# A three-block sequence model on one core: the sequence in two halves, one behind the other through all blocks

## The chip, the cores and the metric

The kernel runs on one core of a Trainium2 chip. The metric is the device time of one execution in microseconds (us). Inputs and weights lie in device memory (HBM). All arithmetic is in float32; the large products split both factors into a high and a low part of the type fp32r and add three products (high·high, high·low, low·high).

## The reference

The input has 1024 tokens of 1024 channels; 16 learned tokens go in front (1040 columns in the kernel's transposed layout). Two layers (a mixer, then a feed-forward block) and a second block follow:

```python
for layer in range(DEPTH):                       # DEPTH = 2
    h = rms_norm(hs, norm_mix_pre[layer])
    if layer < N_A_LAYERS:                       # layer 0: windowed means, grouped product
        mix = pool_mixer(h, pool_w[layer], pool_scale[layer])
    else:                                        # layer 1: window of 128 tokens, 16 heads, 2 key heads
        mix = sliding_window_attention(h, k_blk, v_blk, w_q[j], ...)
    hs = hs + rms_norm(mix, norm_mix_post[layer])
    h = rms_norm(hs, norm_ffn_pre[layer])
    hs = hs + rms_norm(swiglu(h, w_gate_up[layer], w_down[layer]), norm_ffn_post[layer])   # 2816 hidden
x = hs[:, N_META:]
p = (x * (1 + scale) + shift) @ w_in             # scale, shift, gate from silu(c) @ w_ada
out_a = _gmlp_branch(p[..., :1536], ...)         # spatial product within chunks of 128 tokens
out_b = _rwkv7_branch(p[..., 1536:], ...)        # a recurrence over all tokens, 8 heads
o = concatenate([out_a, out_b]) @ w_out
x = _layer_norm(ALPHA * x + gate * o, ln_g, ln_b)
```

Every step is causal: a token needs only itself and tokens before it. The attention needs the keys and values of the 128 tokens before a block of 128 queries, the pooling up to 15 tokens before, the token shift of the recurrent branch one token before, and the recurrence a state of 64x64 numbers per head.

## The kernel before

Channels lie on partitions (eight row blocks of 128), tokens on columns. The columns go in three chunks: 448, 336 and 256 wide in layer 0 (`CH0`), 432, 336 and 256 in layer 1 and the second block (`CH1`).

The class `K` emits the program from Python generators ("threads"). A thread yields a waiting time in ns of TensorE time (`self.t`, advanced by `mm` with a price for each matmul), an event to wait for, or slots of a counted resource to take; `run` always goes on with the ready thread of highest priority. TensorE executes in the order of emission; the other engines are ordered around it by a planner that works with estimated durations, where `soon(n)` puts instructions up to n places ahead.

`split_weight` loads one unit of weights (128x1024, 512 KB) and cuts it: ScalarE (ACT) copies to the high part (L300), VectorE (DVE) subtracts for the low part (L301); with a gain it takes eight instructions on each. `mm3` multiplies: per row block three matmuls of 128x128 weights with one chunk of columns, 24 for a product over eight row blocks, all recorded at L248.

`main` runs the stages one after the other, each over all columns:

- `mixer0`: band products that take windowed means, grouped products. It spawns for each chunk a `finish` thread.
- `finish` (a thread per chunk): the norm of a block's output, the residual, the split of the next input and the sums of the next norm. Its ends are the events `x..` (next input is there) and `s..` (its scales are there). Its instructions run on DVE, ACT and GpSimd (POOL), with a few small products (tiles `st_`, `sb_`).
- `ffn`: for each of 22 column blocks of the hidden layer `up` multiplies gate and up weights with every chunk (tiles `pg`, `pu`), forms silu(gate)·up (L536 to L543) and cuts it; `down` multiplies pairs of column blocks (tile `pd`) and DVE adds the products up (L565).
- `attention`: keys, values and queries; four threads `attend` take two query blocks each: logits, softmax, transposes, product with the values; then the output projection. The next feed-forward block starts when the first chunk's `finish` is through.
- `second`: 29 column blocks of the input product (`shifted`, `gmlp_gemm`), written to HBM; beside them the thread `gmlp` and two threads `rwkv`, which run eight batches `rwkv_half` (a pair of heads, 512 tokens each): small products with waits between them, an inversion by 15 steps on DVE, a chain over eight states. Then the output product, first 512 tokens first, the layer norm (`final`, and `tail_step`/`tail_end` for the last 256 tokens).

Tiles of products in PSUM come from two pools: `pg` with three buffers, `pss` with five. Weights have three sets of high and low parts.

Of the kernel before, what the change touches and what calls it, by code (L numbers as in the profile page):

```python
# [17 lines left out]
D = 1024  # L18
KT = 8
T = 1024  # L20
TB = 5
# [8 lines left out]
CH0 = [(0, 448, 112), (448, 336, 112), (784, 256, 128)]  # L30
CH1 = [(16, 432, 108), (448, 336, 112), (784, 256, 128)]
CH2 = [(16, 512, 128), (528, 512, 128)]
# [79 lines left out]
def const_arrays():  # L112
# [33 lines left out]
# waits of the threads between two blocks: for the sum of squares of each chunk, its spread, a row block  # L146
# (per column), the split, the next sum of squares, its spread
WAIT = {
# [7 lines left out]
# row blocks whose sums (of squares of the output, of the residual, of the next squares) go to the vector engine  # L156
# [7 lines left out]
# instructions that PSUM reads and norms are moved ahead  # L164
# [4 lines left out]

class K:  # L170
    """Emits the program. Threads are generators that yield how long their next step has to wait
    (ns of tensor-engine time), an event to wait for, or slots to take; the tensor engine runs in
    the order of emission, the other engines are scheduled around it."""

    def __init__(self, tc, A, out):
        self.tc, self.nc, self.A, self.out = tc, tc.nc, A, out
        self.t = 0.0
        self.events = set()
        self.res = {}
        self.threads = []  # L180

    # ---- threads
# [18 lines left out]
    def run(self):  # L201
        while self.threads:
            best = None
            for th in self.threads:
                if th[3] is not None and th[3][0] == "acq" and th[1] > self.t:
                    continue
                if th[1] <= self.t and (best is None or th[2] > best[2]) and (th[3] is None or self.can(th)):
                    best = th
# [20 lines left out]
    def eng(self, name, i, k):  # L229
        return self.nc.vector if VECTOR[name][i] >> k & 1 else self.nc.gpsimd  # L230

    def soon(self, n):
        """what is emitted inside goes before what was emitted up to n instructions earlier"""
        return self.tc.high_priority(offset=n)

    # ---- instructions of the tensor engine
    def mm(self, out, lhsT, rhs, start=True, stop=True):
# [4 lines left out]
        if lhsT.dtype == F32R:  # L242
            self.t += max(n / 2.4, 106.0 if m > 64 else 66.0) + 2
# [4 lines left out]
        self.nc.tensor.matmul(out, lhsT, rhs, start=start, stop=stop)  # L248

    def tp(self, out, src, n=128):  # L250
        self.t += 107.0
        self.nc.tensor.transpose(out, src, self.eye[:n, :n])  # L252

    def mm3(self, ps, units, w, first=True, last=True):
        """ps += sum over units (wh, wl, col, xh, xl) of the three products"""
        n = len(units)
        for i, (wh, wl, col, u, v) in enumerate(units):
            a, b = wh[:, col:col + 128], wl[:, col:col + 128]
# [3 lines left out]
            yield 0  # L262

    # ---- tiles
    def act(self, name, dt=F32):
        return self.ap.tile([128, TM], dt, tag="act", name=name)

    def tt(self, name, dt=F32):
        return self.sp.tile([128, 512], dt, tag="t", name=name, bufs=TB)

    def rbt(self, name):
        if self.rp is not None:
            return self.tt(name)
        return self.sa.tile([128, 448], F32, tag="rb", name=name, bufs=5)
# [14 lines left out]
    def split_weight(self, src, name, gain=None, tags=None):  # L289
# [3 lines left out]
        nc.sync.dma_start(out=raw, in_=src)  # L293
        if tags is None:
            h = self.wp.tile([128, 1024], F32R, tag="wh", name=f"wh_{name}", bufs=self.wbufs)
            l = self.wp.tile([128, 1024], F32R, tag="wl", name=f"wl_{name}", bufs=self.wbufs)
        else:
            h, l = [p.tile([128, 1024], F32R, tag=tag, name=f"w{i}_{name}") for i, (p, tag) in enumerate(tags)]
        if gain is None:
            nc.scalar.activation(out=h, in_=raw, func=AF.Copy)  # L300
            nc.vector.tensor_tensor(out=l, in0=raw, in1=h.bitcast(F32), op=ALU.subtract)  # L301
        else:
            for k in range(KT):
                c, g = slice(128 * k, 128 * k + 128), self.v(gain, k)
                nc.scalar.activation(out=h[:, c], in_=raw[:, c], func=AF.Copy, scale=g)
                nc.vector.scalar_tensor_tensor(out=l[:, c], in0=raw[:, c], scalar=g, in1=h[:, c].bitcast(F32), op0=ALU.mult, op1=ALU.subtract)
        return h, l

    def xin(self, X, k, ch, ci):
        """high and low part of row block k of X in the columns of ch, which lie in X's chunk ci"""  # L310
        c0, w, _ = ch
        o = c0 - X["ch"][ci][0]
        return X["h"][k][:, c0:c0 + w], X["l"][ci][k][:, o:o + w]

    def xunits(self, w, X, ch, ci):
        return [(w[0], w[1], 128 * k, *self.xin(X, k, ch, ci)) for k in range(KT)]

    def low(self, name, ci, dt=F32R):
# [1285 lines left out]
```

## Time and profile before

| | us |
|---|---|
| median of 3 executions | 2793.87 (2793.48 to 2807.92) |
| span of the profiled execution, first to last instruction | 2784.2 |
| TensorE (PE) busy in it | 2626.8 (94%) |
| VectorE busy | 1553.5 (56%) |
| ScalarE busy | 923.5 (33%) |
| GpSimd busy | 354.3 (13%) |

PE is busy nearly all the time, so what counts is where it is not, and where its clock is not the full one: "PEclk" in a view by stages is the mean clock that was granted, 1.00 for 2.4 GHz and 0.50 for 1.2 GHz. A busy PE is not a PE at its best: matmuls are pipelined, so the duration of one (about 0.3 us) is longer than the distance to the next. What a matmul costs in a row of matmuls is read from the starts.

### The profile page before, as it was taken

The page shows a single profiled execution, that of the slowest core. Times are in us where ns is not written, and L with a number is a line of the kernel's source. Part 1 is how long each engine was busy: PE and PEld are TensorE (multiplying, and loading weights), DVE is VectorE, ACT ScalarE, POOL GpSimd, SP SyncE. Part 2 cuts the span into 40 slices and gives each one's busy share as a digit, 9 for nine tenths or more (in the row PEclk, how much of TensorE's full clock was granted, in tenths as well). Part 3 has the DMA queues.
Part 4 walks back from the last instruction along what each step waited for, and adds up shares of the span by engine and source line. Part 5 has one row for each costly group of instructions (what it writes and reads, how often), then busy time and mean ns, then how long its engine had stood idle before and what let it go on. Part 6 is the DMA issues. An engine that isn't in the chain of part 4 may idle for free.

```text
span 2784.2 us, 47171 instructions
## 1 busy us (share of the span) xinstructions
PE 2626.8 (94%) x19004; PEld 2446.8 (88%) x19004; DVE 1553.5 (56%) x3397; ACT 923.5 (33%) x1937; POOL 354.3 (13%) x364
## 2 busy tenths in 40 slices
PE   7799999999997899989999999999899999989887
PEld 6699999999997888989999999999798887778666
DVE  6844555454458677465244444455746466464666
ACT  5432111111124577643311111112533334243344
POOL 3500000000005100051000000000301112131235
PEclk9899999999998999989999999999999999999898
DMA  6222222421123110131111111112333222233352
GB/s 207 103 84 76 77 76 70 65 80 46 38 80 104 50 36 32 61 110 65 46 46 46 46 46 46 54 46 79 124 104 96 70 91 82 75 112 98 100 168 87
DMA packets 141243, 217.52 MB, mean 78 GB/s; under 512 B 43129, under 2 KB 96171, under 8 KB 141025
## 3 DMA queue, kind: packets, MB, share of 16 engines
q1 hardware_dynamic: 111296, 178.08, 19.6%
q10 hardware_dynamic: 29728, 36.43, 4.4%
q8 instruction: 149, 2.44, 0.4%
q14 instruction: 70, 0.57, 0.1%
HBM read 169.22 MB, written 45.23 MB: 77 GB/s over the span
## 4 chain that ended last, share of the span: by engine, by line
PE 47%; DVE 7%; issue 6%; POOL 3%; ACT 3%; DMA 2%; SPq 1%; ACTq 0%; DVEq 0%; POOLq 0%
PE pg L248 9%; PE pu L248 8%; PE pd L248 8%; PE po L248 4%; PE pq L248 3%; PE pv L248 2%; PE y L248 1%; PE pr L248 1%; PE S L248 1%; PE qk L248 1%; PE pk L248 1%; PE pgg L248 1%; PE pt L252 1%; PE pgv L248 1%; PE A L248 1%
## 5 line engine op out<-in xcount | busy, mean ns | idle before, releaser
L248 PE MATMUL pu<-xl_a,wh_u 128*128 128x256 f32 (+3 forms) x1056 | 339.7, 322 | 0.0
L248 PE MATMUL pg<-xl_a,wh_g 128*128 128x256 f32 (+3 forms) x1056 | 338.1, 320 | 0.0
L248 PE MATMUL pd<-hh,w_d 128*128 128x256 f32 (+3 forms) x1056 | 324.2, 323 | 7.9 <-ACT hh L542 7.9
L565 DVE TENSOR_TENSOR acc<-pd,acc 128x256 f32<-128x256 f32 (+3 forms) x480 | 240.9, 514 | 148.1 <-PE pd L248 147.9
L539 DVE TENSOR_TENSOR fu<-pu,rb_na 128x448 f32<-128x448 f32 (+1 forms) x132 | 67.9, 515 | 283.7 <-PE pu L248 283.7
L248 PEld LDWEIGHTS pd<-hh,w_d 128*128 128x128 f32 x1056 | 199.6, 191 | 12.8 <-ACT hh L542 8.7
L248 PEld LDWEIGHTS pu<-xl_a,wh_u 128*128 128x128 f32 x1056 | 201.0, 190 | 3.9
L248 PEld LDWEIGHTS pg<-xl_a,wh_g 128*128 128x128 f32 x1056 | 200.3, 190 | 4.4
L368 POOL TENSOR_TENSOR sqf<-sqf,sq 128x336 f32<-128x336 f32 (+3 forms) x21 | 22.6, 1074 | 1403.4 <-ACT sq L367 1396.4
L248 PE MATMUL pg<-oh,wh_g 128*128 128x432 f32 (+2 forms) x624 | 199.7, 320 | 0.0
L248 PE MATMUL pg<-oh,wl_g 128*128 128x432 f32 (+2 forms) x624 | 198.8, 319 | 0.0
L542 ACT ACTIVATE hh<-fg 128x448 fp32r<-128x448 f32 (+1 forms) x132 | 64.7, 491 | 369.2 <-DVE fg L540 367.4
L248 PE MATMUL pd<-hl,w_d 128*128 128x448 f32 (+3 forms) x528 | 170.5, 323 | 2.9 <-DVE hl L543 2.9
L248 PE MATMUL pg<-xh_a,wl_g 128*128 128x448 f32 (+2 forms) x528 | 171.1, 324 | 2.0 <-DVE wl_g L301 2.0
L248 PE MATMUL pg<-xh_a,wh_g 128*128 128x448 f32 (+2 forms) x528 | 172.2, 326 | 0.0
L248 PE MATMUL pu<-oh,wh_u 128*128 128x432 f32 (+2 forms) x528 | 170.2, 322 | 1.8 <-DVE fg L536 1.8
L248 PE MATMUL pu<-xh_a,wh_u 128*128 128x448 f32 (+2 forms) x528 | 171.5, 325 | 0.2 <-DVE fg L536 0.2
L248 PE MATMUL pu<-xh_a,wl_u 128*128 128x448 f32 (+2 forms) x528 | 170.5, 323 | 0.0
L248 PE MATMUL pd<-hh,wh_d 128*128 128x448 f32 (+3 forms) x528 | 170.5, 323 | 0.0
L248 PE MATMUL pu<-oh,wl_u 128*128 128x432 f32 (+2 forms) x528 | 169.3, 321 | 0.0
L248 PE MATMUL pd<-hl,wh_d 128*128 128x448 f32 (+3 forms) x528 | 168.9, 320 | 0.0
L248 PE MATMUL pd<-hh,wl_d 128*128 128x448 f32 (+3 forms) x528 | 168.6, 319 | 0.0
(501 smaller groups left out, 6685.7 us busy)
## 6 DMA issues: line engine op xcount, KB each, us to landing
wr_g<-in_wgu_dram SPq DMA_DIRECT2D x44, 512.0 KB, 3.2
wr_u<-in_wgu_dram SPq DMA_DIRECT2D x44, 512.0 KB, 3.2
wr_d<-in_wdn_dram SPq DMA_DIRECT2D x44, 512.0 KB, 3.2
ada<-in_w_ada_dram ACTq DMA_DIRECT2D x48, 256.0 KB, 2.6
wr_wo<-in_wout_dram SPq DMA_DIRECT2D x16, 512.0 KB, 5.0
xt<-in_hs_tok_dram SPq DMA_DIRECT2D x9, 512.0 KB, 6.2
wr_q<-in_wq_dram SPq DMA_DIRECT2D x8, 512.0 KB, 4.1
wr_wo<-in_wo_dram SPq DMA_DIRECT2D x8, 512.0 KB, 3.1
```

What stands on the lines that cost most here:

```text
L248: self.nc.tensor.matmul(out, lhsT, rhs, start=start, stop=stop)
L252: self.nc.tensor.transpose(out, src, self.eye[:n, :n])
L368: (eng or nc.gpsimd).tensor_tensor(out=acc[:, :w], in0=acc[:, :w], in1=sq[:, :w], op=ALU.add)
L539: nc.vector.tensor_tensor(out=u, in0=pu[:, :w], in1=sb, op=ALU.mult)
L542: nc.scalar.activation(out=hh[:, o], in_=g, func=AF.Copy)
L565: nc.vector.tensor_tensor(out=o, in0=p[:, :w], in1=o, op=ALU.add)
```

## The change

The columns are cut into two halves, A (528 columns with the 16 learned tokens) and B (512). In layer 0 half A goes in two chunks of 264; everything else goes in one chunk of 512 per half.

```diff
-CH0 = [(0, 448, 112), (448, 336, 112), (784, 256, 128)]
-CH1 = [(16, 432, 108), (448, 336, 112), (784, 256, 128)]
+H0 = (((0, 264, 88), (264, 264, 88)), ((528, 512, 128),))
+H1 = (((16, 512, 128),), ((528, 512, 128),))
+NT = 67
+WSETS = 4
```

`main` runs the feed-forward blocks of A, then of B, layer by layer. What lies between two feed-forward blocks of a half runs as a thread of higher priority, and so between the products of the other half's feed-forward block:

```diff
     def main(self):
...
-        yield from self.mixer0(X)
+        yield from self.mixer0((X["a0A"], X["a0B"]))
         self.spawn(self.modulation(), 0.5)
-        yield from self.ffn(0, X, CH0, ("g_fpost0", None, self.hsd[0], self.hsd[1], Xb))
-        yield from self.attention(Xb, Xa)
-        yield from self.ffn(1, Xa, CH1, self.tail2)
-        yield from self.second()
+        self.spawn(self.attentions(X), 1)
+        yield from self.ffn(0, X["a0A"], H0[0], ("g_fpost0", None, self.hsd[0], self.hsd[1], X["b0A"]))
+        yield from self.ffn(0, X["a0B"], H0[1], ("g_fpost0", None, self.hsd[0], self.hsd[1], X["b0B"]))
+        yield from self.ffn(1, X["a1A"], H1[0], ("g_fpost1", "mod", self.hsd[2], self.hsd[3], X["b1A"]))
+        yield from self.ffn(1, X["a1B"], H1[1], ("g_fpost1", "mod", self.hsd[2], self.hsd[3], X["b1B"]))
+        yield from self.second(1, X["b1B"])
+        yield from self.out_second()
+
+    def attentions(self, X):
+        yield from self.attention(0, X["b0A"], X["a1A"])
+        yield from self.attention(1, X["b0B"], X["a1B"])
...
+        self.res.update(early=1, AR=3, S=2, T=NT - 52)
+        self.spawn(self.out_first(), -1)
+        yield from self.second(0, X["b1A"])
```

So the second half of the layer 0 mixer runs beside the feed-forward block of A in layer 0, the attention of A beside that of B in layer 0, the attention of B beside that of A in layer 1, and the second block of A (`second(0)`, its `rwkv` and `gmlp` threads) beside that of B in layer 1. `out_first`, the output product of A, has a priority below the main thread until `second(1)` starts, and one above it from there.

With it come these parts:

- Each unit of weights is loaded and cut once per half. It is asked for at the start of its product; its load is placed behind the last product that used its set. There are four sets. A slot `ring` lets one large product (or one group of a block's products) go at a time, so two threads don't mix theirs.

```diff
+            self.nw += 1
+            dep = self.freed[self.nw - WSETS - 1] if self.nw > WSETS else None
+        ld = nc.sync.dma_start(out=raw, in_=src)
+        if dep is not None:
+            self.after(ld, dep)
```

- Nearly all tiles come from one pool of 67 tiles of 528 columns; a counter `T` of them admits the threads of the second block: 15 for one `rwkv` batch, which gives back 4 and 10 on its way, 5 for a step of `gmlp`, 28 for `out_first`.
- `mm3` yields after its last matmul instead of after every three, so a thread gets in between products only. A `down` takes all its products from the pool `pg`.
- silu in the feed-forward block, except in A's of layer 0, is formed with Tanh, which takes one more DVE instruction:

```diff
+                        nc.scalar.activation(out=u, in_=g, func=AF.Tanh, scale=0.5)
+                        nc.vector.scalar_tensor_tensor(out=g, in0=u, scalar=1.0, in1=g, op0=ALU.add, op1=ALU.mult)
+                        nc.vector.scalar_tensor_tensor(out=u, in0=pu[:, :w], scalar=0.5, in1=sb, op0=ALU.mult, op1=ALU.mult)
```

- `rwkv` is one thread per pair of heads and half; slot `early` lets one at a time through its first part (to the bonus product `bn`). The waiting times of the threads are longer (an inversion 36000 ns instead of 27000, a step of the chain of states 1500 instead of 350), and stores that ACT's queue issued are issued by SP's queue.
- Keys and values of A's last 128 tokens are kept for B, as is the column that the token shift needs and the state of the recurrence.

## Rows read from the trace of the kernel before

**Rows 1.** The page: span, busy time (share) and instructions per engine, DMA in all

```profile
span 2784.2 us, 47171 instructions
PE 2626.8 (94%) x19004; PEld 2446.8 (88%) x19004; DVE 1553.5 (56%) x3397; ACT 923.5 (33%) x1937; POOL 354.3 (13%) x364
DMA packets 141243, 217.52 MB, mean 78 GB/s; under 512 B 43129, under 2 KB 96171, under 8 KB 141025
```

**Rows 2.** Windows by stage: length, busy us (instructions) per engine, clock, DMA, GB/s

```profile
0.00:130.00 130.00, 91.48 (x523) 84.32 (x524) 101.96 (x173) 70.47 (x143) 63.04 (x65) 0.88 0.46 156
130.00:800.00 670.00, 668.00 (x4192) 639.35 (x4191) 317.28 (x539) 132.49 (x208) 0.00 (x0) 1.00 0.23 68
800.00:950.00 150.00, 125.14 (x762) 116.98 (x761) 112.61 (x248) 64.66 (x164) 54.77 (x51) 0.91 0.27 89
950.00:1150.00 200.00, 195.83 (x1753) 174.13 (x1752) 149.18 (x553) 158.81 (x496) 0.00 (x0) 1.00 0.12 41
1150.00:1300.00 150.00, 138.16 (x830) 133.55 (x829) 80.12 (x118) 57.55 (x113) 50.26 (x45) 0.92 0.25 85
1300.00:1950.00 650.00, 650.00 (x4158) 638.04 (x4157) 298.54 (x512) 129.41 (x202) 1.12 (x1) 1.00 0.15 51
1950.00:2050.00 100.00, 86.75 (x528) 82.94 (x527) 68.12 (x140) 47.95 (x94) 26.63 (x31) 0.91 0.37 123
2050.00:2300.00 250.00, 245.11 (x2253) 219.37 (x2252) 139.04 (x406) 80.52 (x152) 29.02 (x35) 0.97 0.28 86
2300.00:2700.00 400.00, 366.69 (x3607) 301.53 (x3605) 229.00 (x611) 141.29 (x271) 89.08 (x86) 0.95 0.35 107
2700.00:2784.20 84.20, 59.67 (x415) 56.60 (x415) 57.65 (x105) 40.36 (x96) 40.38 (x51) 0.86 0.28 90
```

**Rows 3.** Timeline of PE: first and last start of rows of large matmuls, 448 and 512 wide

```profile
403.93 0.37 PE L248 MATMUL pd<-hh,wh_d 128*128 128x448 f32 x1
...
404.96 0.36 PE L248 MATMUL pd<-hh,w_d 128*128 128x448 f32 x1
...
2639.68 0.40 PE L248 MATMUL po<-ohl,wl_wo 128*128 128x512 f32 x1
...
2643.15 0.40 PE L248 MATMUL po<-ohl,wl_wo 128*128 128x512 f32 x1
```

**Rows 4.** Groups by line of DVE and ACT, feed-forward block, window 1400 to 1900

```profile
L565 DVE TENSOR_TENSOR acc<-pd,acc 128x432 f32<-128x432 f32 x64 | 38.8, 607 | 37.3 <-PE pd L248 37.3
L301 DVE TENSOR_TENSOR wl_u<-wr_u,wh_u 128x1024 fp32r<-128x1024 f32 x15 | 18.4, 1226 | 4.3 <-ACT wh_u L300 4.2
L543 DVE TENSOR_TENSOR hl<-fg,hh 128x432 fp32r<-128x432 f32 x14 | 8.5, 609 | 8.8 <-ACT hh L542 8.8
L300 ACT ACTIVATE wh_u<-wr_u 128x1024 fp32r<-128x1024 f32 x15 | 15.9, 1061 | 19.5 <-PE pu L248 11.7 <-PE pg L248 7.8
```

**Rows 5.** The same of DVE, window 840 to 940, norms on POOL

```profile
L408 DVE TENSOR_TENSOR xl_b<-acc,xh_a 128x448 fp32r<-128x448 f32 x8 | 9.1, 1134 | 0.4 <-ACT xh_a L407 0.4
L565 DVE TENSOR_TENSOR acc<-pd,acc 128x336 f32<-128x336 f32 x8 | 3.9, 497 | 0.3 <-PE pd L248 0.3
```

**Rows 6.** Groups of DVE, second block: one product of 512 columns read from PSUM

```profile
L1223 DVE TENSOR_TENSOR U<-U,U 128x512 f32<-128x512 f32 x8 | 5.5, 689 | 1.4 <-PE U L248 1.4
```

**Rows 7.** DMA issues: KB each, us from issue to landing

```profile
wr_g<-in_wgu_dram SPq DMA_DIRECT2D x44, 512.0 KB, 3.2
wr_wo<-in_wout_dram SPq DMA_DIRECT2D x16, 512.0 KB, 5.0
```

**Rows 8.** Waits of PE, longest first in total

```profile
PE sb_pa L252 <- DVE dg_pa L343: 16.1, 3, 8.4
PE pool L248 <- DVE wj L463: 13.3, 2, 11.5
```

**Rows 9.** Timeline of PE: the last recurrent batch, first and last product

```profile
2570.30 0.69 PE L248 MATMUL zw<-wd,wup 64*128 64x512 f32 x1
...
2693.53 0.66 PE L252 MATMUL yo<-eye,yt 128*128 128x128 f32 x4 [2.88 <-DVE yt L1325]
```

More of the change, by code (lines that the diff above doesn't have):

```diff
@@ L315, in xunits @@
-    def xunits(self, w, X, ch, ci):
-        return [(w[0], w[1], 128 * k, *self.xin(X, k, ch, ci)) for k in range(KT)]
-    def low(self, name, ci, dt=F32R):
-        return self.lp.tile([128, CH0[ci][1]], dt, tag=f"l{ci}", name=name)
+                nc.scalar.activation(out=h[i][:, c], in_=r[:, c], func=AF.Copy, scale=g)
+                nc.vector.scalar_tensor_tensor(out=l[i][:, c], in0=r[:, c], scalar=g, in1=h[i][:, c].bitcast(F32), op0=ALU.mult, op1=ALU.subtract)
+        return Weights(h, l)
@@ L505, in mixer0 @@
+        y = []
+        for ci, ch in enumerate(H0[0]):
+            nm = f"0{ci}"
+            s = slice(ch[0] - H0[0][0][0], ch[0] - H0[0][0][0] + ch[1])
+            sq = self.ht(f"sqy0_{nm}")
+            sp = band(ch, nm, 0)
             for gi in range(4):
[L506 to L507 removed]
+                nx = band(ch, nm, gi + 1) if gi < 3 else None
+                yield from product(y, ch, nm, s, gi, sp, sq)
@@ new lines, in last, with attention, scaled, kv_out @@
+            self.done(len(fs))
+            self.res["ring"] += 1
+        yield from up(0)
+        for f in range(1, NF - 2, 2):
+            yield from up(f)
+            yield from up(f + 1)
+            yield from down([f - 1, f])
+        yield from up(NF - 1)
+        yield from last([NF - 2, NF - 1])
+    def attention(self, h, X, Xn):
+        nc, A, xp = self.nc, self.A, self.xp
+        kh, kl, vt = self.kh, self.kl, self.vt
+        q0, nq, _ = H1[h][0]
+        nm = X["name"]
+        if h == 0:
+            yield ("ev", "at0")
+        for ci in range(len(H0[h])):
+            yield ("ev", f"s{nm}_{ci}")
+        b8, pad, sink, rd = self.b8, self.pad, self.sink, self.rd
+        vT = self.ht(f"vT{h}")
+        if h == 0:
+            vT0 = xp.tile([128, 128], F32, tag="vT0", name="vT0")
+            for t in (kh, kl):
+                nc.vector.memset(t[:, :112].bitcast(F32), 0.0)
+            nc.vector.memset(vT0, 0.0)
+        else:
+            for t in (kh, kl):
+                nc.vector.tensor_copy(t[:, :128], t[:, 512:640])
+            nc.vector.tensor_copy(vt[:, 0], vt[:, 4])
+        kb = 112 - H0[0][0][0] if h == 0 else 128 - H0[1][0][0]
+        qf, qs, o_t, oh, ol = [None] * 8, {}, [None] * 8, [None] * 8, [None] * 8
+        def scaled(out, p, c0, w):
+            for ci, (a, n, _) in enumerate(H0[h]):
+                lo, hi = max(a, c0), min(a + n, c0 + w)
+                if lo < hi:
+                    nc.vector.tensor_tensor(out=out[:, lo - c0:hi - c0], in0=p[:, lo - c0:hi - c0], in1=X["s"][ci][:, lo - a:hi - a], op=ALU.mult)
+        def kv_out(which, p, ch):
+            c0, w, _ = ch
@@ new lines, in attention @@
+        blocks = [vT0] if h == 0 else []
+        blocks += [vT[:, H1[h][0][0] - X["base"] + 128 * b:H1[h][0][0] - X["base"] + 128 * b + 128] for b in range(4)]
+        p = self.pss(f"pvt{h}")
+        for j, src in enumerate(blocks[:4]):
+            self.tp(p[:, 128 * j:128 * j + 128], src)
+        j0 = 0 if h == 0 else 1
+        nc.scalar.activation(out=vt[:, j0:j0 + 4], in_=p.rearrange("p (a b) -> p a b", b=128), func=AF.Copy)
+        if h == 0:
+            p = self.pss("pvt0b")
+            self.tp(p[:, :128], blocks[4])
+            nc.scalar.activation(out=vt[:, 4], in_=p[:, :128], func=AF.Copy)
@@ new lines, in attention @@
+            self.events.add(f"q{i}{h}")
+        for k in range(8):
+            yield ("ev", f"o{k}{h}")
+        yield 2500
+        O = dict(h=oh, l=ol, base=q0)
+        y = []
+        sq = self.ht(f"sqo{h}")
+        for m in range(8):
+            yield ("acq", "ring", 1)
+            w2 = self.split_weight(A["wo"][m], f"wo{m}{h}")
+            p = self.pg(f"po{m}{h}")
+            yield from self.mm3(p, self.xunits(w2, O, q0, nq), nq)
+            self.done()
+            self.res["ring"] += 1
+            y.append(self.ht(f"yo{m}{h}"))
+            o = y[m][:, :nq]
+            nc.scalar.activation(out=o, in_=p[:, :nq], func=AF.Identity, bias=self.v("b_o", m))
+            self.sq_add(sq, o, nq, m == 0, self.eng("a1", 0, m))
```

1270 lines of the change are left out of this document (615 added, 655 removed), and 4 rows, old and new, of the table WAIT.

## The prediction

> **What bounds the kernel now.** The page comes first: TensorE (PE) is busy in 94% of the span, VectorE (DVE) in 56%, ScalarE (ACT) in 33% [rows 1]. So the question is what PE loses, and in which stage. The windows by stage tell it [rows 2]. I count as lost what a stage is long minus PE's busy time multiplied by the granted clock. In order of time this gives 49.5 us in the layer 0 mixer and the start of the first feed-forward block (0 to 130: 130 − 91.48 × 0.88), 2.0 in that block, 36.1 where it goes over into the attention (800 to 950), 4.2 within the attention, 22.9 where the attention goes over into the second feed-forward block, 0 in that, 21.1 where it goes over into the second block, 12.2 in its first third (products and recurrent batches mixed), 51.6 while the batches run out of products beside them (2300 to 2700), and 32.9 in the last 84 us. The sum is 232.5; the rest, 2784.2 − 232.5 = 2551.7 us, is work on PE. Time of matmuls that only wait at half clock beside an idle PE is counted a little twice, so 232 is rather an upper value.
>
> What the work costs is next. Six matmuls of 448 columns start 1.03 us apart from first to last (0.206 each, 0.460 ns a column), fifteen of 512 take 3.47 us (0.231 each, 0.452 ns a column) [rows 3]. A column costs the same in a wide chunk as in a narrower one, so 512 instead of 432, 336 and 256 buys nothing, and the work stays 2552 us. All that the change can win is in the 232 us of losses.
>
> **The change part by part.** I go through the losses and say what is left of each; the other work (feed-forward products) stays as it is.
>
> *Start, 49.5.* Half A's mixer needs half the norm work before the first feed-forward products, and in 0 to 130 DVE is busy 102 us [rows 2], which is the bound there. But the first PE instruction waits 11.5 us for its data in any case [rows 8], and the chain of norm, spread and split (8.4 us for one spread alone [rows 8]) is a latency that two chunks have as three had. I take 40, between 30 (DVE's part halved) and 50 (nothing won).
>
> *The two transitions around the attention and the attention, 36.1 + 22.9 + 4.2.* These go under 371 us of the other half's feed-forward products (22 blocks × 72 matmuls × 512 columns × 0.457 ns). The thread has time enough: norm 45, products 57, softmax batches about 150, output product 45, norm 40, together some 340 us, and its stage lasts 371 + 152 us of PE work. What it costs there is the loss of mixed work, 4.2 us per 200 in the attention now [rows 2]: I keep 4 (0 to 12).
>
> Cover by DVE must be asked, since the stage has both loads. A feed-forward block of 512 columns takes per hidden block 4 sums and 5 other operations of 0.69 us [rows 6] and 3 cuts of 1.23 [rows 4]: 9.9 us in 16.9 us of PE. 22 of them are 218 us; half the attention with its norms and weights is about 167. That is 385 us in 523, or 74%. Now DVE is at 75% (149.18 of 200) between 950 and 1150 while PE runs at 98% [rows 2], so this load is hidden.
>
> *Weights twice.* 181 units more are loaded and cut: 222 us more of DVE (1.23 each), 192 of ACT (1.06) [rows 4]; the Tanh form adds 66 DVE instructions, 45 us. DVE comes to 1821 us, 67% of the new span. Transfers rise by 95 MB to 312 MB, or 115 GB/s from 78 [rows 1], where the stage 0 to 130 moves 156 [rows 2]. A unit now lasts 24 × 0.234 = 5.6 us instead of 11.4. With four sets the shortest lead is a pair of products, 11.2 us, and a unit needs 3.2 to 5.0 us for its transfer [rows 7] and 2.3 for both cuts, so 4 to 6 us are spare in SP's, ACT's and DVE's queues. I take 0. What stands on SP's queue in front of a load (stores of the norm, of `shifted` and `gmlp`, the 27 small transfers of a recurrent batch) can take that spare time; then PE waits for the rest of it.
>
> *Norms beside products.* Six `finish` threads now run beside the other half's products. While POOL works, DVE's subtraction of 448 columns from two SBUF tiles takes 1134 ns [rows 5]; one of 432 without POOL takes 609 [rows 4]. The sum from PSUM stays at 497 for 336 columns [rows 5]. So the split is slowed, the evacuation of PSUM is not. I take 2.5 us a norm, 15 in all, between 0 and 35.
> The Trainium skill, page "SBUF — State Buffer", section "Who interferes with whom", says the same more sharply: a DVE instruction with two SBUF inputs and a GpSimd instruction that reads SBUF fully block each other. It speaks against this change, which puts POOL's norm work beside feed-forward products whose silu, split and cuts all have two SBUF inputs; by it the 15 would be nearer 35, and the sum 20 us higher.
>
> *Recurrent batches.* Between 2050 and 2300, with products beside them, 12.2 us go with three of the eight batches, 4 each [rows 2]. A's four batches run beside 371 + 163 us of products: 16 us (0 to 40). By the slots for tiles they go one, later two at a time, some 180 us each, so they are done shortly before the feed-forward block of B ends. B's four have 163 us of products, and the slots `early` and `T` start them about 45 us apart; the last one starts, by my count, 230 us after the end of the feed-forward block and needs 123 us as the last one does now [rows 9], while the products end at 300. So some 55 us at the end have only the remains of two batches and of `gmlp` to do. I take 4 × 4 + 34 = 50, between 25 and 80; it was 51.6 for five batches.
>
> *Third transition, 21.1.* `out_first` (8 products, 45 us) is held for just this gap. Its loads and cuts have to run first, beside the norm: 10 (5 to 21).
>
> *End, 32.9.* The last 512 columns go in two parts of 256 as now, with the same last norm: 33 (27 to 40).
>
> *Chunks of 264* cost 0.004 ns more per column than those they replace, 3 us over 836 thousand columns.
>
> Sum of what is lost: 40 + 4 + 16 + 15 + 50 + 10 + 33 + 3 = 171. The span is 2552 + 171 = 2723. The median lies 9.7 us above the profiled span (2793.9 against 2784.2), a start and end that no stage shows. That makes 2732; I say 2730. With all low ends (30, 0, 0, 0, 25, 5, 27) it is 2649, with all high ends (50, 12, 40, 35, 80, 21, 40) 2842.
>
> **The rivals.**
>
> *Slower: DVE is late for PSUM.* A product of `down` has six matmuls, 1.4 us, and needs one sum of 0.69 us by DVE; its pool has three buffers and nothing else now. A cut (1.23), an attention operation or a slowed split in front of it in DVE's queue, which runs in order, holds PE as soon as two products are behind. There are 4 × 11 × 8 = 352 such products. Lost 0.22 us at each (78 us) the kernel is at 2808, half a percent slower than now; at 0.3 it is at 2836. For it: the new stages have DVE at 74%, POOL beside it, and products only a third as long as a chunk-triple was. Against: between 950 and 1150 the same DVE share costs 2%, and DVE now waits 37.3 us for PE before 64 of the 432-wide sums [rows 4], so sums are not late.
>
> *Little won: the recurrence becomes the path.* If A's batches are not done when B's feed-forward block ends, `out_first` can't fill the gap (11 us more) and holds tile slots, so that B's last batches start 30 to 40 us later. This gives about 2775. For it: about 50 us of margin in a count of 600; against: the waits in the count are the change's own, longer than the present ones.
>
> *More won: only start and end lose.* Losses of 30 + 5 + 5 + 10 + 30 + 30 give 2552 + 110 + 10, about 2670. For it: the stretches 130 to 800 and 1300 to 1950 lose 2 us in 1320 [rows 2]; against: every stretch with small steps loses 2 to 5%.
>
> **How the numbers follow.** Forecast (2690 to 2770) 0.48, more won 0.17, recurrence as path 0.15, DVE late 0.20. The smallest change that a measurement of this kernel can tell is about 0.5%, 14 us: faster is below 2780, slower above 2808. The forecast, the second case, two thirds of the third and a tenth of the last lie below: 0.77, I say 0.76. A quarter of DVE late and the rest of the recurrence case are within: 0.09. Slower 0.15. The range leaves out the lower third of the case with more won and the worse half of DVE late: 2660 to 2815.
>
> **What would show it.** Right: PE busy 50 of 50 us in windows from about 90 to the end of the third feed-forward pass, clock 1.00 there, losses left in the first 80 us and the last 150; DVE at about 67%, its splits slower, its sums not; 197 + 181 loads of weights. Wrong: idle time of PE before `pd` or `pg` put down to the sums, to the cuts `wl_` or to a weight's transfer, spread over all stages; a gap between the last feed-forward product and the first of `second(1)` in which `out_first` does not run; recurrent steps that PE waits for in the middle passes.

## The result and the profile after

The changed kernel takes 2838.86 us (median of four, 2835.32 to 2842.23) against 2798.84 for the kernel before in the same runs: 1.0143 times, interval 1.0112 to 1.0175. It is slower; 2730 was predicted, with 2815 as the upper end. The profiled execution spans 2837.6 us, 53 more than before, 115 more than the predicted span of 2723.

Page of the changed kernel:

```profile
span 2837.6 us, 41913 instructions
...
PE 2629.9 (93%) x16381; PEld 2183.1 (77%) x16381; DVE 1745.2 (62%) x3366; ACT 1068.7 (38%) x1996; POOL 348.2 (12%) x324
...
DMA packets 156885, 314.57 MB, mean 111 GB/s; under 512 B 44792, under 2 KB 68778, under 8 KB 156688
```

PE and the transfers (312 MB, 115 GB/s forecast) are close to what the prediction said, DVE is 4% under it (1821 forecast). So the loss must be read by stages again, as in [rows 2]. Windows of the changed kernel, columns as there; the ends are the ends of the feed-forward passes (558, 1116, 1664, 2362):

```profile
0.00:142.00 142.00, 97.06 (x660) 92.65 (x661) 78.87 (x165) 63.67 (x141) 36.15 (x48) 0.87 0.38 125
142.00:300.00 158.00, 130.13 (x887) 122.96 (x887) 90.89 (x139) 51.28 (x82) 23.40 (x17) 0.87 0.54 142
300.00:558.00 258.00, 255.82 (x2041) 250.57 (x2040) 156.89 (x294) 70.18 (x112) 8.24 (x10) 0.99 0.37 116
558.00:1116.00 558.00, 538.54 (x2734) 432.34 (x2733) 359.94 (x710) 242.00 (x517) 52.17 (x44) 0.98 0.31 99
1116.00:1664.00 548.00, 529.68 (x2645) 426.26 (x2644) 355.94 (x674) 236.98 (x493) 45.21 (x29) 0.98 0.31 101
1664.00:2362.00 698.00, 671.29 (x4198) 526.29 (x4196) 411.82 (x763) 221.71 (x333) 66.62 (x70) 0.98 0.35 110
2362.00:2420.00 58.00, 53.74 (x222) 43.35 (x223) 43.59 (x50) 31.54 (x45) 23.17 (x14) 0.91 0.57 192
2420.00:2678.00 258.00, 248.31 (x2041) 196.87 (x2040) 171.44 (x420) 106.68 (x178) 53.49 (x54) 0.98 0.40 126
2678.00:2837.60 159.60, 105.33 (x966) 91.80 (x964) 75.87 (x155) 44.62 (x99) 39.76 (x40) 0.75 0.28 87
```

Lost, as length minus PE's busy time times clock, against what was forecast (the 15 us for six norms stand in one line here, though one of the six lies in pass 1 and one in pass 4):

| stage | lost | forecast |
|---|---|---|
| start, 0 to 142 | 57.6 | 40, with the next line |
| second half of the mixer beside the first products, 142 to 300 | 44.8 | |
| rest of the first pass, to 558 | 4.7 | 0 |
| attention and norms beside passes 2 and 3, 558 to 1664 | 59.1 | 19 |
| second block of A beside pass 4, 1664 to 2362 | 40.1 | 16 |
| third transition, to 2420 | 9.1 | 10 |
| second block of B and end | 95.3 | 83 |

The last two lines lie within their ranges. The first two lost 62 us more than forecast, passes 2 and 3 lost 40 more, pass 4 lost 24 more. (The sum is 310.7, and 2526.9 is left as work, 25 less than before. The clock has two digits only: half a digit on 2630 us of busy PE is 13 us in each of the two traces, so a good part of these 25 us can be rounding.)

What PE waits for (waits of PE, longest in total first: us, times, longest):

```profile
PE pua0A L265 <- DVE fg L599: 15.9, 3, 6.6
PE po L265 <- ACT oc L1403: 15.2, 3, 8.1
...
PE st_pa0A L265 <- DVE sqy L392: 11.3, 1, 11.3
PE pda0B L265 <- DVE fg L599: 10.8, 6, 3.3
PE pda1A L265 <- DVE fg L599: 7.8, 4, 3.0
...
PE po L265 <- DVE fu L602: 7.4, 1, 7.4
PE pga0A L265 <- DVE wl_ga0A L330: 6.0, 1, 6.0
```

`fg` is DVE's first read of a gate product from PSUM (the line after `pg` in `up`). A product `pd` or `pu` that waits for it waits for a buffer: three products stand in the pool and the oldest has not been read. Two such places. In the start (timeline, PE and DVE; in brackets the idle time before and what ended it):

```profile
166.10 1.23 DVE L330 TENSOR_TENSOR wl_ga0A<-wr_ga0A,wh_ga0A 128x1024 fp32r<-128x1024 f32 x1 [11.59 <-ACT wh_ga0A L329]
...
179.11 1.28 DVE L922 SCALAR_TENSOR_TENSOR moda<-ada,silu_c,moda 128x1024 f32<-128x1024 f32 x1 [10.78 <-DMA ada<-in_w_ada_dram]
180.31 0.43 DVE L602 TENSOR_TENSOR fu<-pua0A,rb_na0A 128x264 f32<-128x264 f32 x1
...
180.88 0.77 PE L265 MATMUL po<-ph,wh_pw1B 128*128 128x512 f32 x1 [7.42 <-DVE fu L602]
```

DVE stands 11.6 us at the head of its queue for a weight and 10.8 us for a tile of the modulation; the reads `fg` and `fu` stand behind, and PE behind them. The transfers come late because of one that I had not looked at (issues, 140 to 175 us: KB each, us from issue to landing):

```profile
reld<-band ACTq DMA_DIRECT2D x1, 3072.0 KB
wr_ga0A<-in_wgu_dram SPq DMA_DIRECT2D x1, 512.0 KB, 18.2
```

This is the attention's bias table, broadcast to HBM. It runs at some 96 GB/s from 142 to 173 us, the DMA engines are 90% busy there, and a unit of weights takes 18.2 us instead of 3.2 [rows 7]. And within pass 2:

```profile
795.81 0.68 DVE L766 TENSOR_TENSOR ol<-o,oh 128x512 fp32r<-128x512 f32 x1
796.41 0.68 DVE L599 TENSOR_TENSOR fg<-pga0B,rb_na0B 128x512 f32<-128x512 f32 x1
...
797.14 0.69 PE L265 MATMUL pda0B<-hha0B,wh_da0B 128*128 128x512 f32 x1 [2.03 <-DVE fg L599]
```

Here softmax instructions and a split of the attention stand ahead of `fg`, DVE works without a break, and PE waits 2 us. Of the ten waits for `fg` of more than 1 us in passes 2 and 3, four (8.1 us together) look like this. In the other six (15.9 us) it is the products, sums and splits of a norm that stand there, many of them slowed beside POOL: before the wait of 2.8 us that ends at 1047 us two splits took 1.53 and 1.75 us.

### The profile page after: what moved, and what is told of

Same layout as the page of the kernel before. It is cut to its first block, busy times and chain, and to the rows that moved or that the text cites. A ratio compares the mean times of both kernels' runs of the same rounds, so it can differ in the third digit from the quotient of the medians.

```text
span 2837.6 us, 41913 instructions
## 1 busy us (share of the span) xinstructions
PE 2629.9 (93%) x16381; PEld 2183.1 (77%) x16381; DVE 1745.2 (62%) x3366; ACT 1068.7 (38%) x1996; POOL 348.2 (12%) x324
## 4 chain that ended last, share of the span: by engine, by line
PE 72%; DVE 12%; issue 5%; DMA 4%; ACT 3%; POOL 3%; SPq 1%; DVEq 0%; POOLq 0%; ACTq 0%
PE po L265 6%; PE pda0A L265 5%; PE pua0A L265 4%; PE pga0A L265 4%; PE pda1A L265 4%; PE pua1A L265 4%; PE pda0B L265 4%; PE pga0B L265 4%; PE pua0B L265 3%; PE pga1A L265 3%; PE pq L265 3%; PE pga1B L265 3%; PE pua1B L265 3%; PE pda1B L265 2%; PE pv L265 2%
## 5 line engine op out<-in xcount | busy, mean ns | idle before, releaser
L265 PE MATMUL pua0A<-xh_a0A,wh_ua0A 128*128 128x264 f32 x352 | 106.2, 302 | 15.9 <-DVE fg L599 15.9
L265 PE MATMUL po<-oc,wh_wo 128*128 128x256 f32 (+1 forms) x384 | 94.4, 339 | 17.1 <-ACT oc L1403 15.2
L265 PE MATMUL pda0A<-hha0A,wh_da0A 128*128 128x264 f32 x352 | 105.0, 298 | 4.9 <-DVE acca0A L627 4.2
L265 PE MATMUL pga0A<-xh_a0A,wl_ga0A 128*128 128x264 f32 x352 | 102.1, 290 | 6.0 <-DVE wl_ga0A L330 6.0
L265 PE MATMUL pga0A<-xh_a0A,wh_ga0A 128*128 128x264 f32 x352 | 103.3, 294 | 2.6 <-ACT xh_a0A L435 2.6
L265 PE MATMUL pua0A<-xh_a0A,wl_ua0A 128*128 128x264 f32 x352 | 104.8, 298 | 0.0
L265 PE MATMUL pua0A<-xl_a0A,wh_ua0A 128*128 128x264 f32 x352 | 104.7, 297 | 0.0
L265 PE MATMUL pga0A<-xl_a0A,wh_ga0A 128*128 128x264 f32 x352 | 102.4, 291 | 0.5 <-DVE xl_a0A L439 0.5
L265 PE MATMUL pda0A<-hla0A,wh_da0A 128*128 128x264 f32 x352 | 102.0, 290 | 0.0
L265 PE MATMUL pda0A<-hha0A,wl_da0A 128*128 128x264 f32 x352 | 101.9, 289 | 0.0
L265 PE MATMUL pda0B<-hha0B,wh_da0B 128*128 128x512 f32 x176 | 75.3, 428 | 15.2 <-DVE fg L599 10.8
L265 PEld LDWEIGHTS po<-oc,wh_wo 128*128 128x128 f32 x384 | 68.5, 203 | 25.5 <-ACT oc L1403 15.9
```

What stands on the lines that cost most here:

```text
L265: self.last = self.nc.tensor.matmul(out, lhsT, rhs, start=start, stop=stop).ins
```

## The experiments

Each runs beside the kernel before on the same chip; "changed" is the changed kernel, 2838.9 us. It was not run again beside them; the kernel before was, and its median went from 2797.0 to 2802.8, so a difference of 6 us between runs that did not stand side by side says nothing. Theory: three separate prices, the broadcast in the start, late reads of PSUM with too few buffers, and POOL's sums that hold DVE up. Where a gain sits is read from the passes, worked out from the end of the last `pd` of each in the timeline (us):

| profiled run | pass 1 | pass 2 | pass 3 | pass 4 | rest |
|---|---|---|---|---|---|
| changed | 558.3 | 557.9 | 548.1 | 697.7 | 475.6 |
| e1_bias_late | 550.6 | 558.4 | 546.9 | 698.6 | 479.0 |
| f2_bias_pieces | 564.1 | 568.8 | 546.1 | 702.7 | 475.4 |
| g2_bias_rows | 534.7 | 557.3 | 548.5 | 697.4 | 475.7 |
| e2_psum44 | 550.7 | 545.5 | 537.0 | 691.0 | 474.9 |
| e3_pool_off | 553.1 | 549.5 | 544.4 | 692.1 | 475.4 |
| g1_combo_rows | 528.5 | 539.8 | 531.3 | 686.8 | 475.9 |

**e1_bias_late: the table behind the modulation.**

```diff
     def modulation(self):
         yield 60000
-        yield from self.biases()
...
         nc.vector.tensor_scalar(out=self.mod[:, 8:16], ...)
+        yield from self.biases()
         self.events.add("at0")
```

> One edit of the changed kernel: the bias table of the attention (with its 3 MB broadcast to HBM, `reld`) is made behind the modulation, as in the kernel before, instead of ahead of it, where it lay at 141 us. Theory (the broadcast fills the DMA engines from 142 to 173 us, the weights `wr_ga0A` and `wr_ua0A` and the modulation's `ada` come late, and DVE and ACT stand at their heads with the reads of PSUM behind them): the gaps of PE at 163, 173, 203 and 231 us go, the loss of the window 142 to 300 falls from 44 us to under 15, and the time falls by 25 to 40 us, to 2800 to 2815. Rival (the loss there is the second half of the mixer, its norm on DVE and POOL, beside the first blocks): the gaps stay, the time falls by less than 10 us.

2836.7 us (1.0141, 1.0098 to 1.0183): nothing measurable in all. But the loss moved:

```profile
142.00:290.00 148.00, 131.96 (x967) 126.31 (x967) 99.38 (x158) 50.98 (x80) 24.26 (x17) 0.94 0.42 143
290.00:550.00 260.00, 245.25 (x1944) 238.77 (x1943) 147.25 (x274) 67.92 (x109) 7.32 (x9) 0.98 0.43 120
```

24.0 us are lost where it was 44.8, and 19.7 in the rest of the pass where it was 4.7: the loss goes with the broadcast. In the kernel before it lies in the feed-forward block too (issued at 532 us), and a window round it shows 2 us lost:

```profile
500.00:570.00 70.00, 68.00 (x424) 63.69 (x424) 30.02 (x56) 11.37 (x18) 0.00 (x0) 1.00 0.52 81
```

**f2_bias_pieces and g2_bias_rows: the same in 16 pieces of 192 KB.**

```diff
-        nc.scalar.dma_start(out=self.rd, in_=band.unsqueeze(1).to_broadcast([16, 128, 384]))
+        for a in range(16):
+            # f2: one head each
+            self.after(nc.scalar.dma_start(out=self.rd[a:a + 1], in_=band[a:a + 1].unsqueeze(1).to_broadcast([1, 128, 384])))
+            # g2: eight rows of all heads each, instead
+            self.after(nc.scalar.dma_start(out=self.rd[:, 8 * a:8 * a + 8], in_=band.unsqueeze(1).to_broadcast([16, 8, 384])))
+            yield 8000
```

> The changed kernel with the bias table behind the modulation in 16 broadcasts of 192 KB, 8 us apart. In the run with the one broadcast moved there, the loss went with it: 19 us less from 142 to 290, 12 more from 290 to 550. Theory (30 us in which the broadcast holds the DMA engines are more than the lead of the weights; pieces of 2 us are within it): nothing lost from 290 to 550, the time 12 to 20 us below that of the changed kernel, 2818 to 2828. Rival (the transfers are too many in all, whatever their order): as that run, 2833 to 2840.

2858.9 us (1.0198, 1.0165 to 1.0231): 20 us slower than the changed kernel, a miss on both sides; the pieces go out until 616 us, and passes 1 and 2 are the longer ones. A piece that is one head comes from one partition, and took 8.9 us to land (issues of f2 from 430 to 560 us, then those of g2 from 400 to 560):

```profile
reld<-band ACTq DMA_DIRECT2D x13, 192.0 KB, 8.9
```

```profile
reld<-band ACTq DMA_DIRECT2D x15, 192.0 KB, 3.3
```

> The changed kernel with the bias table alone, behind the modulation, in 16 pieces of 8 rows of all heads. Theory: nothing lost to it from 290 to 550 us, 2815 to 2825. Rival (any further transfer beside weights that are loaded twice takes their lead): 2830 to 2845.

2817.3 us (1.0063, 1.0040 to 1.0087), 21.6 less than the changed kernel, all of it in pass 1. Nothing is left of the broadcast (windows of g2):

```profile
142.00:290.00 148.00, 131.69 (x964) 125.97 (x964) 99.61 (x157) 51.34 (x81) 24.31 (x17) 0.94 0.43 143
290.00:535.00 245.00, 243.61 (x1951) 237.85 (x1949) 148.36 (x276) 68.52 (x109) 6.77 (x8) 1.00 0.42 121
```

So it is not the number of bytes (they are the same in all), but how long they hold the DMA engines in one go: 30 us, or 8.9 us again and again, cost what 3.3 us do not.

**e2_psum44: a fourth buffer for the large products.**

```diff
-            self.ps = P("psg", 3, space=PSUM)
-            self.p2 = P("pss", 5, space=PSUM)
+            self.ps = P("psg", 4, space=PSUM)
+            self.p2 = P("pss", 4, space=PSUM)
```

> One edit of the changed kernel: the pool of the large products has four PSUM buffers instead of three, the other pool four instead of five. Theory (from 558 us on PE waits because DVE reads the large products late, and the fourth product behind has no buffer): the waits of `pd` for `fg` and for the sums, 45 us in the trace from 540 to 2360 us, fall to under 15, with the half clock behind them the time falls by 25 to 45 us, to 2795 to 2815. Rival (the attention and the recurrence need their five buffers, or DVE is late by more than one product): no gain, 2830 to 2860.

2804.9 us (1.0031, 1.0008 to 1.0053), 34.0 less. Passes 2 and 3 win 12 and 11 us, 1 and 4 win 7 each. In passes 2 and 3 the waits for `fg` fell from 26.2 to 6.1 us, those for sums from 5.2 to 1.7. In the changed kernel, 558 to 1664 us, these are the two lines of `pda0B` and `pda1A` above (10.8 and 7.8) and

```profile
PE pua1A L265 <- DVE fg L599: 4.4, 3, 2.2
PE pua0B L265 <- DVE fg L599: 3.2, 1, 3.2
PE pda1A L265 <- DVE acca1A L627: 3.1, 3, 1.1
...
PE pda0B L265 <- DVE acca0B L627: 2.1, 2, 1.0
```

And in e2, 558 to 1640 us:

```profile
PE pv L265 <- DVE am L794: 5.7, 6, 2.3
PE pda0B L265 <- DVE fg L599: 4.7, 4, 1.9
...
PE pda1A L265 <- DVE fg L599: 1.4, 2, 1.1
PE pda1A L265 <- DVE acca1A L627: 1.3, 1, 1.3
...
PE pda0B L265 <- DVE acca0B L627: 0.4, 1, 0.4
```

The first of these lines is new: the attention's product `pv` waits, 5.7 us in all, since the fourth buffer was taken from the other pool.

**e4_prio400: the reads moved further ahead in the planner's order.** `PRIO = 50` becomes 400.

> One edit of the changed kernel: the reads of PSUM by the feed-forward block are moved up to 400 instructions ahead by the planner instead of up to 50. Theory (they are late since the attention's and the recurrence's instructions stand ahead of them in DVE's queue): the waits of `pd` for `fg` and sums fall by half, the time falls by 10 to 25 us. Rival (they stand where the planner thinks PE will have finished, so the order hardly changes, or DVE now waits for PE at the head of its queue): within 10 us of the changed kernel.

2833.2 us (1.0139, 1.0093 to 1.0184): no difference that can be told. In passes 2 and 3 the waits for `fg` fell to 17.7 us and those for sums rose to 11.8: what one read gains in DVE's queue the other loses. The buffer helped, this order did not.

**e3_pool_off: no sums on POOL in the norms beside products.** The masks `VECTOR` of `b0`, `a1` and `b1` are all ones.

> One edit of the changed kernel: in the norms behind the attention and behind the feed-forward blocks (not in that of the layer 0 mixer) the sums that POOL makes go to DVE. Theory (POOL's sums hold DVE up while they run: a split of 512 columns takes 1.6 us beside them against 0.69): DVE gets 0.7 us for each sum more and loses the 0.9 us a split, the gaps of PE of 2 to 3.5 us at about 597, 601, 1044, 1157 and 1590 us go, and the time falls by 5 to 15 us. Rival (DVE's queue is what is late, whoever makes it so): DVE has 60 more instructions and the time rises by 5 to 20 us.

2818.8 us (1.0087, 1.0054 to 1.0119), 20.1 less, a little over the expected end. Groups of the norm, 1000 to 1075 us, of the changed kernel and of e3:

```profile
L424 DVE SCALAR_TENSOR_TENSOR yo<-yo,vecs,rb_pa1A 128x512 f32<-128x512 f32 x8 | 9.3, 1191 | 0.4 <-ACT rb_pa1A L378 0.4
L439 DVE SCALAR_TENSOR_TENSOR xl_a1A<-yo,vecs,xh_a1A 128x512 fp32r<-128x512 f32 x8 | 8.8, 1111 | 0.4 <-ACT xh_a1A L435 0.4
...
L425 POOL TENSOR_TENSOR yo<-yo,old_a1A 128x512 f32<-128x512 f32 x5 | 8.0, 1621 | 9.0 <-DVE yo L424 4.8 <-DMA old_a1A<-hsd 4.2
```

```profile
L439 DVE SCALAR_TENSOR_TENSOR xl_a1A<-yo,vecs,xh_a1A 128x512 fp32r<-128x512 f32 x8 | 5.9, 742 | 0.0
L424 DVE SCALAR_TENSOR_TENSOR yo<-yo,vecs,rb_pa1A 128x512 f32<-128x512 f32 x8 | 5.8, 740 | 0.4 <-ACT rb_pa1A L378 0.4
L425 DVE TENSOR_TENSOR yo<-yo,old_a1A 128x512 f32<-128x512 f32 x8 | 5.4, 678 | 0.0
```

And on its page:

```profile
PE 2617.6 (93%) x16381; PEld 2169.8 (77%) x16381; DVE 1741.5 (62%) x3451; ACT 1067.8 (38%) x1996; POOL 234.8 (8%) x239
```

DVE does 85 instructions more and is busy 3.7 us less. The 113 us that POOL worked on them spared DVE nothing. In passes 2 and 3 the waits for `fg` are 15.9 us for 26.2.

**f1_combo and g1_combo_rows: the three edits together** (POOL's sums now also out of the mixer's second half and its norm; f1 with pieces of one head, g1 with pieces of eight rows).

> The changed kernel with three edits at once: four PSUM buffers for the large products, no sums on POOL in the norms that lie beside products (now the second half of the layer 0 mixer too), and the bias table behind the modulation in 16 broadcasts of 192 KB, 8 us apart, instead of one of 3 MB. Theory (the three causes are distinct: buffers 34 us, POOL's sums 20, the broadcast and POOL in the start 25 to 35, with some overlap between the first two): 2755 to 2785, below the kernel before. Rival (buffers and POOL are one and the same wait, already gone with four buffers): 2785 to 2800.

2808.5 us (1.0033, 1.0016 to 1.0050), outside what either side expected: pass 2 took 562.6 us, with PE idle 13 and 10 us at 569 and 600 while the slow pieces ran.

> As the run with the three edits at once, but the table goes out in 16 pieces that each take 8 of the 128 rows of all 16 heads. There a piece was one head, read from one partition, and ran at 27 to 30 GB/s against 96 of the single broadcast, so 192 KB held the DMA engines 7 us instead of 2, and PE stood 13 and 10 us at 569 and 600 us. Theory (pieces of 2 us fit into the lead of the weights): the loss of 290 to 1086 us, 56 us there, comes down to 25, the time to 2770 to 2785, below the kernel before. Rival (it is not the broadcast but the sums of the norm, now on DVE, that hold PE at 569 and 600): 2800 to 2810.

2763.0 us (0.9869, 0.9841 to 0.9898): 75.9 less than the changed kernel, where the three edits alone gave 34.0, 20.1 and 21.6, in all 75.7. That the two are so near is partly chance: the profiled runs alone gave 38.5, 23.1 and 23.9, in all 85.5, and together 75.2, and g1 also takes POOL out of the mixer's second half, which no run does by itself. So there are three prices which share some 10 us at most by these traces, as buffers and POOL's sums do where a slowed split stands ahead of `fg`. Without them the kernel in halves is 1.3% faster than the kernel before. Its windows, 142 us to the end of pass 4:

```profile
142.00:290.00 148.00, 135.93 (x1026) 130.34 (x1025) 105.03 (x178) 54.13 (x84) 2.03 (x2) 0.97 0.44 143
290.00:528.50 238.50, 235.71 (x1886) 231.33 (x1885) 144.94 (x279) 66.91 (x108) 1.76 (x1) 0.99 0.45 126
528.50:1068.30 539.80, 530.54 (x2732) 427.09 (x2732) 357.28 (x747) 240.77 (x515) 4.67 (x5) 1.00 0.33 104
1068.30:1599.60 531.30, 522.22 (x2645) 421.20 (x2644) 352.64 (x699) 237.09 (x493) 4.03 (x4) 1.00 0.32 104
1599.60:2286.40 686.80, 664.80 (x4197) 523.54 (x4195) 412.00 (x768) 220.85 (x333) 55.54 (x63) 0.99 0.35 112
```

Passes 2 and 3 now lose 9.3 and 9.1 us (30.2 and 28.9 in the changed kernel), 142 to 290 loses 16.1, pass 4 28.6.

**h1_before_both: two of the edits in the kernel before** (four buffers each, the same masks).

> The kernel before with two of the three edits that help the changed kernel: four PSUM buffers for the large products and four for the others, and no sums on POOL in the norms behind the attention and the feed-forward blocks. Theory (both are prices of work that lies beside other products; in the kernel before the norm lies bare and DVE is early for the feed-forward sums): no gain, the transitions get longer with more on DVE, 2798 to 2825. Rival (both would have helped either kernel, so they are no cost of the change): 15 us faster or more, below 2785.

2789.6 us (0.9963, 0.9944 to 0.9983): 10 us faster, between theory and rival. So of the 54 us that these two edits gave one by one about 44 belong to the change. Against this kernel g1 is at 2763.0/2789.6 = 0.990.

**f3_attn_alone: the attention not beside products.** Halves as in the change, but `main` waits.

```diff
         yield from self.ffn(0, X["a0A"], ...)
+        yield ("ev", "sa1A_0")
         yield from self.ffn(0, X["a0B"], ...)
+        yield ("ev", "sa1B_0")
```

> The changed kernel with the attention of each half no longer beside the feed-forward products of the other: the main thread waits for the attention of a half and its norm before it goes on, the rest stays in two halves. Theory (to lie beside products is worth what the transitions cost, the change wins there and gives back in the reads of PSUM): each half shows its two transitions of some 35 and 20 us and 10 to 20 us within the attention, 130 to 150 us of loss from 558 to 1664 against 53 in the changed kernel, time 2905 to 2945. Rival (lying beside products wins little, since DVE is then late): below 2880.

3036.5 us (1.0838, 1.0790 to 1.0886), 198 slower, far beyond what I expected (windows of the attention of A with the pass behind it, and of B):

```profile
560.00:1200.00 640.00, 551.20 (x2720) 447.25 (x2721) 365.53 (x699) 237.11 (x507) 45.28 (x39) 0.91 0.27 85
1200.00:1523.00 323.00, 219.12 (x1210) 179.93 (x1209) 174.90 (x423) 146.11 (x368) 43.60 (x29) 0.78 0.23 73
```

They lose 138 and 152 us; beside products the same work costs 59. A half alone leaves PE bare; how much of this is due to the waits of these threads, which were made for the overlap, was not tested. In the kernel before, with all columns at once, transitions and attention cost 63 us [rows 2]. So the overlap hides what the cut into halves lays bare, but in the changed kernel it wins only 4 us against before; in g1 it wins some 45.

**f4_rwkv_waits, g3_waits, i3_rwkv_long: the waits in the recurrent batches.** In `rwkv`, half A: the waits ahead of the first products 7500, 6000, 8500 ns become 9500, 8000, 12000 (f4, g3) or 15000, 14000, 20000 (i3), in f4 and g3 a step of the chain 2200 for 1500; in g3 also the last two batches of B 350 for 1500 and 27000 for 36000. f4 stands on the changed kernel, g3 and i3 on g1.

> The changed kernel with longer waiting times in the recurrent batches of half A alone: 9500 for 7500, 8000 for 6000, 12000 for 8500 ns ahead of their first products and 2200 for 1500 in the chain of states. Theory (the 41 us lost from 1664 to 2362 are steps that PE reaches before DVE has their input): the waits of PE there, 27 us, fall under 15 and the time falls by 8 to 20 us. Rival (DVE is as late behind its queue, and the last batch of A now ends behind the feed-forward block): no gain or up to 20 us slower.

2832.5 us (1.0109, 1.0079 to 1.0138). The 6 us lie within the spread, and the waits of PE in pass 4 did not fall (28.2 us in the trace against 26.6): the rival.

> As the first of these, with the longer waits in the recurrent batches of half A (which took 6 us off the changed kernel) and shorter ones in the last two of half B (a step of the chain 350 for 1500 ns, an inversion 27000 for 36000), where the end of the kernel has no products beside them. Theory (the 75 us lost in the last 160 are the chain of the last batch, and the waiting times are part of it): 10 to 25 us below that run. Rival (there PE waits for DVE and for transfers, whatever the waits say): within 8 us of it.

2768.8 us (0.9888, 0.9864 to 0.9911), 6 more than g1: the rival again.

> The run with all three edits, and in half A's recurrent batches the waits ahead of the first products are doubled (7500, 6000 and 8500 ns to 15000, 14000 and 20000). Theory (the waits of PE for `kq`, `BK`, `QM`, 10 to 15 us of the 37 lost, are steps that come too soon): those waits fall under 4 us, and with the half clock behind them 8 to 15 us are won, unless the last batch then ends behind the feed-forward block of B, which it does 55 us ahead now. Rival (what is lost there is not waited for at these steps): within 5 us.

2757.9 us (0.9855, 0.9825 to 0.9885), 5 less than g1, at the border of the rival and within the spread; pass 4 is 681.8 us for 686.8 and the others are the same. The waits for `kq`, `BK` and `QM` are gone, one of 5.9 us for `yt` came.

**i1_pool_second, i2_mixer_later: what else is left in g1.** i1 moves six kinds of POOL's work in the second block to DVE; i2 lets the mixer's second half wait 100000 ns for 10000.

> The run with all three edits (buffers, norms without POOL, table in pieces; 2763 us), and in the second block six kinds of POOL's products and sums of 64x512 to 128x512 go to DVE as well. It still loses 37 us where the second block of half A lies beside the feed-forward block of B, against 16 that I predicted. Theory (POOL holds DVE up there too): 10 to 20 us off that run, the pass of B in layer 1, 687 us long there, becomes 670 to 680. Rival (there POOL runs too seldom, 43 us in 685, and the path of a batch is what counts): within 6 us.

2772.0 us (0.9909, 0.9877 to 0.9941), 9 more, pass 4 693.1 us for 686.8: POOL seems worth having there.

> The run with all three edits, and the second half of the layer 0 mixer waits 100 us of PE time instead of 10 behind the first before it starts, so that it lies in the middle of the feed-forward block of A. Theory (the 15 us lost from 142 to 290 come from two loads on DVE at once: second half and the modulation's first products): the loss there falls under 6, and 5 to 10 us are won in all. Rival (the second half costs what it costs wherever it lies): within 4 us.

2762.9 us (0.9870, 0.9841 to 0.9899): the same as g1. Its trace is of the fastest of its four runs (2754.1; the others took 2761.7 to 2765.2): there pass 1 is 12 us shorter than in g1, passes 2 and 3 are 4 us longer. The medians do not tell the two apart.

## Why the prediction was wrong, point by point

*What bounds the kernel; the work.* Right: the work is 2527 for 2552, part of the difference rounding, and what made the kernel slower are the losses, 311 for 171. The low end of the sum (2649) leaves out the 3 us for narrow chunks that the high end has; that changes nothing here.

*Start, 40: the step that failed most.* I costed the mixer's norms and went over `modulation` as if it had stayed. The change calls `biases` at its head instead of its end, and the broadcast at 141 us meets weights that need 116 GB/s (300 to 558) instead of 68 [rows 2]. g2 puts a price of 22 us on it; in the kernel before it was 2. That a step which is moved takes its DMAs along is just what should have been counted. Besides, two chunks gave no shorter start (57.6 us to 142, 49.5 to 130 before; PE waits 11.3 us for the first norm); no run tested why. And I had the mixer's second half at nothing: the stretch in which it runs, beside the modulation, still loses 16 in g1. i2 did not settle which of the two that is.

*Weights twice, 0.* Right in pass 1, where nothing else is in the way: 4.7 us in its rest, 1.4 in g2. In passes 2 and 3 the cuts, and the instruction that Tanh adds, are part of DVE's load; no run tells what they cost there. The lead of 4 to 6 us fits too, though no run measured it: pieces of the table that land in 3.3 us cost nothing (g2), those of 8.9 us cost more than the whole had (f2). But I named only SP's queue as what could use it up, not a transfer from ACT's queue.

*Attention 4 and norms 15: failed in size and mechanism.* 59 were lost. This is the slower rival, DVE late for PSUM, and its place was nearly right: it is not so much the sums of `down` as the first read of the gate product (26.2 us against 5.2 for sums in the waits), since `down` fills the pool's last buffer. The change had made this pool tighter itself: before, the first two of the eight row blocks of a `down` took their buffers from the other pool. My argument against it was DVE's share: 75% between 950 and 1150 cost 2% [rows 2]. In passes 2 and 3 the share is 65%, less than the 74% that I had counted, and still the loss is 5%. The share says nothing on how long a burst stands ahead of one read; with three buffers PE waited 31.4 us behind such bursts, with four 7.8 (e2). With the edits of g1 passes 2 and 3 together lose 18.4. That this is near the 19 of the forecast is chance: 15 of the 19 were for norms slowed by POOL, and g1 has none.

*Norms and POOL.* I took the row where the sum from PSUM stayed at 497 ns [rows 5] for proof that the evacuation isn't slowed. The single read isn't; it stands behind splits that are (1111 ns for 742), and that is where the row was read too narrowly. e3 gives the price of POOL's sums beside products: 20.1 us where I had 15. The rule of the Trainium skill, page "SBUF — State Buffer", section "Who interferes with whom", had been taken for 35, 20 on top of the 15, so that e3 measured 20 as well is chance. In kind the trace agrees with the rule of the Trainium skill: these splits, with both inputs in SBUF, are held up, and DVE's sums from PSUM are not (683 ns beside an instruction of POOL, 686 without, 300 to 2362 us).

*Batches of A, 16: failed in size.* 40 were lost, 28.6 in g1. In pass 4 buffers took 7 off and POOL's sums in the norms 6; longer waits little (2 in f4, 5 in i3), and moving POOL's other work made it 6 longer (i1). The "4 a batch" came from three batches beside second block products, which leave DVE more room than feed-forward products (139 of 250 us there [rows 2], 412 of 698 here). That this is the cause is argued, not shown; some 12 us stay open.

*Third transition 10, batches of B 50, end 33.* Right for the first (9.1), and `out_first` ran in the gap as counted; the other two lost 95.3 for 83, within their ranges. No experiment moved the last 476 us.

*Chances.* The rival that came had 0.20. That its price of 2808 to 2836 nearly holds the result is luck: it asked 78 to 106 us for late reads, and buffers and POOL's sums together were worth 54. Each of the two large misses, 62 us in the start and 40 in passes 2 and 3, would have stayed within the range by itself; together they left it, for its upper end was made from one mechanism at a time.

## What to carry to other kernels

Work put beside a busy engine is hidden only if the reads that free its buffers are prompt: look for what can stand ahead of them in the reading engine's queue, and try one more buffer in the product pool (34 us here); an average share doesn't show this. When transfers are raised to hide other work, go through every transfer that was moved as well, and cut the long ones into pieces shorter than the lead. A helper engine that holds the busy one up while it runs may spare it nothing, so compare the busy time of both with and without it (e3), for each kind of work: in the second block moving POOL's work off it won nothing (i1).

## What the runs showed that was not expected

A broadcast from SBUF to HBM ran at about 96 GB/s from 16 partitions and at 26 to 30 GB/s from one (192 KB landed in 8.9 us, 3.3 when eight rows of 16 partitions went). And DVE took 85 sums over from POOL and was busy no longer, 1741.5 us for 1745.2.
